# Hybrid encoder trunk: per-half buffers for the last 1/rms, VectorE evacuation of four FFN tiles, and later splits of one weight and four operands

## Chip, cores and metric

One NeuronCore of one Trainium2 chip runs the whole kernel in one launch. The metric is the device time of an execution in microseconds (us); times inside the program are counted from the start of the profiled span. TensorE is called PE in the rows, VectorE DVE, ScalarE ACT, GpSimd POOL; SP is the queue that issues most DMA transfers. PEld is TensorE's loading of weights.

## What is computed

Two encoder layers over 512 tokens of width 1024 in float32. Only the FFN and the last norm matter here (the reference, cut):

```python
for i in range(DEPTH):                      # DEPTH = 2
    ...                                     # norm, input projection, attention and SSD groups, output projection
    h = rms_norm(x, norm_ffn_w[i])
    g = jnp.einsum("bld,df->blf", h, w_gate[i])
    u = jnp.einsum("bld,df->blf", h, w_up[i])      # D_FF = 2816 = 22 tiles of 128
    x = x + jnp.einsum("blf,fd->bld", jax.nn.silu(g) * u, w_down[i])
return rms_norm(x, final_norm_w)
```

## The kernel before

All products are made in float32r from operands split in two: a high part `h` (a cast by ScalarE) and a low part (VectorE subtracts the high part from the source). A product a·b becomes three matmuls, hi·hi, hi·lo and lo·hi, so each weight chunk needs a `whi` (ACT, line 191) and a `wlo` (DVE, line 192). Weights stream through `Stream`: `next()` hands out one chunk and writes the splits of the two after it, and the load of the third, into the program. Two `wraw` buffers hold raw chunks, so the load of a chunk waits until the `wlo` of the chunk two before it has been made.

The 22 FFN tiles of a layer are worked in four phases, tiles 0 to 3, 4 to 9, 10 to 15 and 16 to 21. The first four (`PLAIN = 4`) are "plain": 24 matmuls of 512 columns for gate and 24 for up each, in PSUM banks a, s, t, s. Their evacuation is `evac`: VectorE multiplies gate by the token scale `rb` (1/rms spread over a tile), ScalarE applies SiLU, GpSimd multiplies the result by `rb` again, VectorE multiplies by up, and the hidden tile is split into `hid` (cast by ACT, line 1011, low part by DVE, line 1012). The tiles `gs` (tag e0) and `a_` (tag e1) have one buffer each. The other 18 tiles go in pairs by a seven-product scheme with sums of weight blocks and sums of the normed input. For that, still during the plain tiles, VectorE makes the normed input `xn` (line 1020, eight instructions), three operands `s11`, `s12`, `s22`, four sums in place (line 1051), and then four summed operands `ss1`, `ss2`, `sn4`, `ss3` (lines 1027 and 1028), which lie in the buffers `xh` and `xl` that the plain tiles' matmuls still read.

At the end of each phase come the down products: eight output tiles m = 0 to 7 in banks a and s by turns, each over the phase's hidden tiles; in the first phase that is 12 matmuls of 512 columns per m (lines 1112 to 1114), and then one add to x (DVE, line 1115).

A scheduler that works from its own times orders the instructions of each engine when the kernel is built; each engine then runs its list strictly in that order, and an instruction that waits holds all behind it. `tc.high_priority()` moves instructions forward in that order; `tc.issue_after(i)` puts them behind i.

The last norm (`Last`) works its last tile in two halves of 256 tokens. Each half's 1/rms is made by `rsqrt` on VectorE (eleven instructions on 128x2 elements, lines 290 to 296) and then applied by ACT (lines 407, 410) and DVE (412) to the output rows; eight DMAs of 256 KB write them out. The result tile of `rsqrt` takes its name as its tag, so two calls with one name share one buffer.

## Time and profile before

| | |
|---|---|
| median of 3 runs | 1213.37 us (1212.6 to 1213.63) |
| the profiled execution's own time | 1212.78 us |
| its span, first to last instruction | 1211.0 us |
| around the span | 1.78 us |
| TensorE busy in the span | 1190.3 us (98%) |
| VectorE, ScalarE, GpSimd busy | 902.2, 633.3, 149.8 us |
| mean granted TensorE clock | 0.995 of full speed |

Sums below are made against the profiled execution (1212.78 us), which lies 0.59 us below the median. A matmul's busy time in the rows overlaps that of the next one, so what TensorE loses is read from the distance of starts, not from the busy share.

### The profile page before, as it was taken

What the parts mean: (1) busy time and instruction counts of PE and PEld (TensorE: products, weight loads), DVE (VectorE), ACT (ScalarE), POOL (GpSimd) and SP (SyncE); (2) the same over time, 40 slices, a digit from 0 to 9 for tenths busy, and PEclk for the clock granted to TensorE, in tenths of its full rate; (3) what the DMA queues carried; (4) which work ended last, traced back from release to release, by engine and by line L of the source; (5) the groups of instructions that cost most, each with busy time, mean ns of one, the idle gap of its engine ahead of it and who ended that gap; (6) DMA issues with size and microseconds to landing.
All of it is one profiled execution on the core that took longest, in us unless ns stands there. A gap on an engine that the chain in (4) does not pass through costs nothing.

```text
span 1211.0 us, 19732 instructions
## 1 busy us (share of the span) xinstructions
PE 1190.3 (98%) x7720; PEld 1056.5 (87%) x7720; DVE 902.2 (75%) x1477; ACT 633.3 (52%) x1208; POOL 149.8 (12%) x140
## 2 busy tenths in 40 slices
PE   9999999999999999999999999999999999999996
PEld 7889887788899899899898888878879989989985
DVE  7999986568886676677779977866688857847842
ACT  5668775344444354254556876844335524533634
POOL 0202432012000000000211053401020000000011
PEclk9999999999999999999999999999999999999998
DMA  6221111225143233231433111312242432332121
GB/s 223 96 75 54 44 53 53 73 84 165 58 135 123 70 122 114 67 100 40 151 126 103 60 35 56 95 33 91 81 146 96 140 105 70 124 108 83 36 79 70
DMA packets 47534, 110.04 MB, mean 91 GB/s; under 512 B 5425, under 2 KB 5937, under 8 KB 47441
## 3 DMA queue, kind: packets, MB, share of 16 engines
q1 hardware_dynamic: 46720, 107.68, 28.0%
q8 instruction: 60, 0.98, 0.3%
q10 hardware_dynamic: 720, 1.11, 0.3%
q14 instruction: 34, 0.27, 0.1%
HBM read 104.44 MB, written 4.33 MB: 90 GB/s over the span
## 4 chain that ended last, share of the span: by engine, by line
PE 89%; DVE 5%; ACT 3%; DMA 1%; issue 1%; POOL 0%; SPq 0%; ACTq 0%; DVEq 0%; POOLq 0%
PE ps_a L1068 6%; PE ps_a L1067 6%; PE ps_a L1066 6%; PE ps_a L419 5%; PE ps_a L420 5%; PE ps_a L421 5%; PE ps_s L1112 3%; PE ps_s L1114 3%; PE ps_s L1113 3%; PE ps_a L1113 3%; PE ps_a L1112 3%; PE ps_a L1114 3%; PE ps_s L1068 3%; PE ps_s L1067 3%; PE ps_s L1066 3%; PE ps_t L729 3%
## 5 line engine op out<-in xcount | busy, mean ns | idle before, releaser
L191 ACT CAST whi<-wraw 128x512 fp32r<-128x512 f32 (+4 forms) x183 | 125.5, 714 | 211.6 <-PE ps_a L420 52.7
L191 ACT CAST whi<-sraw 128x1024 fp32r<-128x1024 f32 x126 | 131.7, 1050 | 141.0 <-DVE sraw L166 40.4
L192 DVE TENSOR_TENSOR wlo<-wraw,whi 128x512 fp32r<-128x512 f32 (+4 forms) x183 | 149.4, 831 | 54.2 <-ACT whi L191 53.1
L192 DVE TENSOR_TENSOR wlo<-sraw,whi 128x1024 fp32r<-128x1024 f32 x126 | 153.6, 1223 | 46.3 <-ACT whi L191 46.1
L328 POOL TENSOR_TENSOR ssq<-ssq,sqt 128x512 f32<-128x512 f32 x17 | 24.9, 1463 | 680.0 <-ACT sqt L325 679.3
L419 PE MATMUL ps_a<-xh,whi 128*128 128x512 f32 x272 | 107.2, 397 | 0.6 <-DVE x L834 0.3
L421 PE MATMUL ps_a<-xh,wlo 128*128 128x512 f32 x272 | 106.6, 392 | 0.0
L420 PE MATMUL ps_a<-xl,whi 128*128 128x512 f32 x272 | 106.3, 392 | 0.0
L166 DVE TENSOR_TENSOR sraw<-sraw 128x1024 f32<-128x1024 f32 x72 | 88.0, 1222 | 1.0
L1068 PE MATMUL ps_a<-ss,wlo 128*128 128x256 f32 x288 | 81.7, 284 | 0.0
L1066 PE MATMUL ps_a<-ss,whi 128*128 128x256 f32 x288 | 81.5, 283 | 0.0
L1067 PE MATMUL ps_a<-ss,whi 128*128 128x256 f32 x288 | 81.5, 283 | 0.0
L1068 PE MATMUL ps_a<-s,wlo 128*128 128x256 f32 x288 | 81.1, 283 | 0.0
L1067 PE MATMUL ps_a<-s,whi 128*128 128x256 f32 x288 | 81.1, 283 | 0.0
L1066 PE MATMUL ps_a<-s,whi 128*128 128x256 f32 x288 | 79.8, 283 | 0.0
L427 PE MATMUL ps_a<-whi,xh 128*128 128x256 f32 (+1 forms) x256 | 74.2, 291 | 0.1
L428 PE MATMUL ps_a<-wlo,xh 128*128 128x256 f32 (+1 forms) x256 | 73.9, 290 | 0.0
L429 PE MATMUL ps_a<-whi,xl 128*128 128x256 f32 (+1 forms) x256 | 71.9, 286 | 0.0
L1113 PE MATMUL ps_a<-hid,whi 128*128 128x512 f32 x176 | 68.9, 391 | 1.7 <-DVE hid L1012 1.7
L1112 PE MATMUL ps_s<-hid,whi 128*128 128x512 f32 (+1 forms) x182 | 70.0, 385 | 0.3 <-DVE a__3261 L1009 0.2
L1113 PE MATMUL ps_s<-hid,whi 128*128 128x512 f32 (+1 forms) x182 | 69.8, 384 | 0.0
L1114 PE MATMUL ps_s<-hid,wlo 128*128 128x512 f32 (+1 forms) x182 | 69.7, 383 | 0.0
(412 smaller groups left out, 3441.7 us busy)
## 6 DMA issues: line engine op xcount, KB each, us to landing
sraw<-in_w_gate SPq DMA_DIRECT2D x72, 256.0 KB, 3.3
sraw<-in_w_up SPq DMA_DIRECT2D x72, 256.0 KB, 4.0
wraw<-in_w_down SPq DMA_DIRECT2D x48, 384.0 KB, 3.2
wraw<-in_w_xbc SPq DMA_DIRECT2D x16, 512.0 KB, 3.2
wraw<-in_w_out SPq DMA_DIRECT2D x16, 512.0 KB, 3.3
wraw<-in_w_q SPq DMA_DIRECT2D x8, 512.0 KB, 3.5
wraw<-in_w_z SPq DMA_DIRECT2D x8, 512.0 KB, 3.3
wraw<-in_w_gate SPq DMA_DIRECT2D x8, 512.0 KB, 3.2
```

Of the source, the lines that this page charges most:

```text
L166: V.tensor_tensor(q[to], q[to], q[by], ALU.add)
L191: A.copy(hi[:, u], raw[:, u])
L192: (G if lo_pool else V).tensor_tensor(lo[:, u], raw[:, u], hi[:, u].bitcast(F32), ALU.subtract)
L419: T.matmul(ps, lhsT=wh, rhs=op.h[k], start=first, stop=False)
L420: T.matmul(ps, lhsT=wh, rhs=op.l[k], start=False, stop=False)
L421: T.matmul(ps, lhsT=wl, rhs=op.h[k], start=False, stop=last)
L1066: T.matmul(out, lhsT=wh[:, o:o + P], rhs=x_[:, 0, i], start=first and i + j == 0, stop=False, skip_group_check=True)
L1067: T.matmul(out, lhsT=wh[:, o:o + P], rhs=x_[:, 1, i], start=False, stop=False, skip_group_check=True)
L1068: T.matmul(out, lhsT=wl[:, o:o + P], rhs=x_[:, 0, i], start=False, stop=i == 3, skip_group_check=True)
L1112: T.matmul(ps[:, cols], lhsT=w1[:, o:o + P], rhs=h, start=f == a, stop=False)
L1113: T.matmul(ps[:, cols], lhsT=w1[:, o:o + P], rhs=g, start=False, stop=False)
L1114: T.matmul(ps[:, cols], lhsT=w2[:, o:o + P], rhs=h, start=False, stop=f == b - 1)
```

## The change

Four edits. The two last calls of `rsqrt` get a name, and so a buffer, each. In `evac`, up is multiplied by `rb` on VectorE (a new instruction from PSUM), GpSimd's product is gone, and VectorE multiplies the two in SBUF; `evac` runs under `high_priority`. The cast of the first down chunk of a layer (`late`) is put behind the cast `W.cast`, which at that point of the program is that of the third plain tile's hidden half. The four operands with a tag that begins with x (`ss1`, `ss2`, `sn4`, `ss3`) are put behind `W.low`, the low part of the fourth plain tile; the built program keeps that for their VectorE halves, while two of their casts on ScalarE stand ahead of the third tile's.

```diff
@@ -99,7 +99,7 @@
         return psum.tile([P, S], F32, name=f"ps_{tag}", tag=tag)
 
 
-    chunks, pairs = [], []
+    chunks, pairs, late = [], [], []
 
     def stream(src, n, lo=0, cut=WU):
 
@@ -130,6 +130,8 @@
                 for what in PRODUCTS:
                     chunks.append((len(pairs) - 1, what, None, WU))
             for m in range(KT):
+                if a == 0 and m == 0:
+                    late.append(len(chunks))
                 stream(w_down[l, m, :, a * P:b * P], (b - a) * P)
 
     class Stream:
@@ -188,7 +190,9 @@
                 lo = wp.tile([P, WU], F32R, name="wlo", tag="wlo", bufs=WB)
                 for a in range(0, n, KVDT if j == 0 else cut):
                     u = slice(a, min(a + (KVDT if j == 0 else cut), n))
-                    A.copy(hi[:, u], raw[:, u])
+
+                    with tc.issue_after(self.cast.ins) if j in late else nullcontext():
+                        A.copy(hi[:, u], raw[:, u])
                     (G if lo_pool else V).tensor_tensor(lo[:, u], raw[:, u], hi[:, u].bitcast(F32), ALU.subtract)
                 self.sp[j] = (hi, lo)
                 self.raw[j] = None
@@ -398,7 +402,7 @@
                 T.matmul(ms[:, c:c + 1], lhsT=q[:, c * P:(c + 1) * P], rhs=inv, start=False, stop=True)
             mm = small(nrm, 2, "mf")
             V.tensor_scalar(mm, ms[:, :2], EPS, None, ALU.add)
-            rt = rsqrt(nrm, mm, 2, "rfin")
+            rt = rsqrt(nrm, mm, 2, f"rfin{i}")
 
             def last(i, o, tp):
                 for c in range(2):
@@ -1002,14 +1006,14 @@
 
             def evac(f, pg, pu, rb):
                 gs = ff.tile([P, S], F32, name="gs", tag="e0")
+                a_ = ff.tile([P, S], F32, name="a_", tag="e1")
                 V.tensor_tensor(gs, pg, rb, ALU.mult)
+                V.tensor_tensor(a_, pu, rb, ALU.mult)
                 A.activation(gs, gs, AF.Silu)
-                G.tensor_tensor(gs, gs, rb, ALU.mult)
-                a_ = ff.tile([P, S], F32, name="a_", tag="e1")
-                V.tensor_tensor(a_, gs, pu, ALU.mult)
+                V.tensor_tensor(a_, a_, gs, ALU.mult)
                 ah, al = (t.rearrange("p a b -> p (a b)") for t in hidden(f))
-                A.copy(ah, a_)
-                V.tensor_tensor(al, a_, ah.bitcast(F32), ALU.subtract)
+                W.cast = A.copy(ah, a_)
+                W.low = V.tensor_tensor(al, a_, ah.bitcast(F32), ALU.subtract)
 
 
             ops, parts = {}, {}
@@ -1024,8 +1028,10 @@
 
             def operand(name, src, pool, tag):
                 t = pool.tile([P, 2, 4, 256], F32R, name=f"s{name}", tag=tag)
-                A.copy(t[:, 0], src)
-                V.tensor_tensor(t[:, 1], src, t[:, 0].bitcast(F32), ALU.subtract)
+
+                with tc.issue_after(W.low.ins) if tag[0] == "x" else nullcontext():
+                    A.copy(t[:, 0], src)
+                    V.tensor_tensor(t[:, 1], src, t[:, 0].bitcast(F32), ALU.subtract)
                 ops[name] = t
 
             for f in range(PLAIN):
@@ -1043,14 +1049,16 @@
                 if f == 0:
                     with tc.high_priority():
                         _, rb = norm.finish()
-                    evac(f, *pp, rb)
+                    with tc.high_priority():
+                        evac(f, *pp, rb)
                     scaled(rb)
                     for i, n in enumerate(("11", "12", "22")):
                         operand(n, parts[n], ff, f"s{i}")
                     for to, x_, y_ in (("22", "21", "22"), ("21", "11", "21"), ("11", "22", "11"), ("12", "12", "11")):
                         V.tensor_tensor(parts[to], parts[x_], parts[y_], ALU.add if to == "12" else ALU.subtract)
                 else:
-                    evac(f, *pp, rb)
+                    with tc.high_priority():
+                        evac(f, *pp, rb)
 
             for n, src, tag in (("s1", "22", "xh1"), ("s2", "11", "xl1"), ("n4", "12", "xh0"), ("s3", "21", "xl0")):
                 operand(n, parts[src], res, tag)
```

How the engines' lists change is shown at three places, all in the first layer; the second layer has the same rows. Line numbers of the changed kernel are 4 to 8 higher. The first place is VectorE's list from the second plain tile's hidden half to the down products, before. `wlo_3197`, `wlo_3228`, `wlo_3279` and `wlo_3299` are the low parts of down chunks m = 0, 1, 2, 3; `a__3190` and `a__3261` are the third and fourth plain tile.

```order
L1012 TENSOR_TENSOR hid_3028<-a__3120,hid_3028 128x512
L1051 TENSOR_TENSOR xn1_3032<-xn0_3031,xn1_3032 128x4x256
L192 TENSOR_TENSOR wlo_3279<-wraw_3231,whi_3278 128x512
L1051 TENSOR_TENSOR xn0_3031<-xn0_3031,xn1_3032 128x4x256
L1009 TENSOR_TENSOR a__3190<-gs_3186,ps_t_3155 128x512
L1005 TENSOR_TENSOR gs_3257<-ps_s_3195,rbc_3020 128x512
L1028 TENSOR_TENSOR ss2_3268<-xn1_3032,ss2_3268 128x1024
L1028 TENSOR_TENSOR ss1_3265<-xn0_3031,ss1_3265 128x1024
L1012 TENSOR_TENSOR hid_3192<-a__3190,hid_3192 128x512
L1028 TENSOR_TENSOR ss3_3274<-xn1_3032,ss3_3274 128x1024
L1009 TENSOR_TENSOR a__3261<-gs_3257,ps_s_3226 128x512
L192 TENSOR_TENSOR wlo_3299<-wraw_3282,whi_3298 128x512
```

There the low parts of m = 0 and 1 stand further up, that of m = 2 stands ahead of the operands, and those of m = 3 between them. The same place in the changed kernel (`a__3258` is the fourth plain tile):

```order
L196 TENSOR_TENSOR wlo_3197<-wraw_3160,whi_3196 128x512
L1011 TENSOR_TENSOR a__3258<-ps_s_3226,rbc_3020 128x512
L196 TENSOR_TENSOR wlo_3228<-wraw_3200,whi_3227 128x512
L1013 TENSOR_TENSOR a__3258<-a__3258,gs_3257 128x512
L1016 TENSOR_TENSOR hid_3192<-a__3258,hid_3192 128x512
L1034 TENSOR_TENSOR ss1_3265<-xn0_3031,ss1_3265 128x1024
L1034 TENSOR_TENSOR ss2_3268<-xn1_3032,ss2_3268 128x1024
L1034 TENSOR_TENSOR sn4_3271<-xn0_3031,sn4_3271 128x1024
L1034 TENSOR_TENSOR ss3_3274<-xn1_3032,ss3_3274 128x1024
L196 TENSOR_TENSOR wlo_3279<-wraw_3231,whi_3278 128x512
L196 TENSOR_TENSOR wlo_3299<-wraw_3282,whi_3298 128x512
L1123 TENSOR_TENSOR x0_2853<-x0_2853,ps_a_3277 128x512
```

All four operands now stand in one piece behind the fourth tile's low part, and the low parts of m = 2 and 3 stand behind all four.

The second place is TensorE's list at the start of the down products, before: `ps_a_3277` is m = 0, `ps_a_3317` is m = 2, `hid_3028` holds plain tiles 0 and 1, `hid_3192` tiles 2 and 3.

```order
L1112 MATMUL ps_a_3277<-hid_3028,whi_3196 128x512
L1113 MATMUL ps_a_3277<-hid_3028,whi_3196 128x512
L1114 MATMUL ps_a_3277<-hid_3028,wlo_3197 128x512
L1112 MATMUL ps_a_3317<-hid_3028,whi_3278 128x512
L1113 MATMUL ps_a_3317<-hid_3028,whi_3278 128x512
L1114 MATMUL ps_a_3317<-hid_3028,wlo_3279 128x512
L1112 MATMUL ps_a_3317<-hid_3028,whi_3278 128x512
L1113 MATMUL ps_a_3317<-hid_3028,whi_3278 128x512
L1114 MATMUL ps_a_3317<-hid_3028,wlo_3279 128x512
```

The first matmul with `wlo_3279` is there the sixth of this piece, and three matmuls of m = 0 stand even before the fourth tile's last ones. In the changed kernel no down matmul stands among the plain tiles; 28 of m = 0 to 3 come first, of which the last six are shown, and then the first with `wlo_3279` (`ps_s_3297` is m = 1, `ps_s_3337` m = 3):

```order
L1121 MATMUL ps_a_3277<-hid_3192,whi_3196 128x512
L1122 MATMUL ps_a_3277<-hid_3192,wlo_3197 128x512
L1121 MATMUL ps_s_3297<-hid_3192,whi_3227 128x512
L1122 MATMUL ps_s_3297<-hid_3192,wlo_3228 128x512
L1120 MATMUL ps_s_3337<-hid_3028,whi_3298 128x512
L1121 MATMUL ps_s_3337<-hid_3028,whi_3298 128x512
L1122 MATMUL ps_a_3317<-hid_3028,wlo_3279 128x512
L1120 MATMUL ps_a_3317<-hid_3028,whi_3278 128x512
L1121 MATMUL ps_a_3317<-hid_3028,whi_3278 128x512
```

The list behind that row holds 67 further matmuls of the phase, which all stand behind it.

The third place is ScalarE's list at the start of the first pair of the second phase, before. `whi_3414` is the chunk of the pair's first product, `e0` the copy that frees bank a for the third one.

```order
L191 CAST whi_3414<-sraw_3396 128x1024
L191 CAST whi_3433<-sraw_3396 128x1024
L1077 COPY e0_3450<-ps_a_3454 128x512
L191 CAST whi_3458<-sraw_3396 128x1024
L191 CAST whi_3487<-sraw_3402 128x1024
L191 CAST whi_3517<-sraw_3399 128x1024
L191 CAST whi_3546<-sraw_3405 128x1024
L1079 COPY e1_3451<-ps_s_3455 128x512
```

And in the changed kernel, where the copy stands three casts further back:

```order
L195 CAST whi_3414<-sraw_3396 128x1024
L195 CAST whi_3433<-sraw_3396 128x1024
L195 CAST whi_3458<-sraw_3396 128x1024
L195 CAST whi_3487<-sraw_3402 128x1024
L195 CAST whi_3517<-sraw_3399 128x1024
L1085 COPY e0_3450<-ps_a_3454 128x512
L195 CAST whi_3546<-sraw_3405 128x1024
L1087 COPY e1_3451<-ps_s_3455 128x512
```

On SP the load of down chunk 2 moves from among the twelve loads of the next phase's blocks (`sraw`) to behind them.

## Rows read from the trace of the kernel before

**Rows 1.** The page: busy time of each engine, and the chain that ended last.
```profile
PE 1190.3 (98%) x7720; PEld 1056.5 (87%) x7720; DVE 902.2 (75%) x1477; ACT 633.3 (52%) x1208; POOL 149.8 (12%) x140
...
PE 89%; DVE 5%; ACT 3%; DMA 1%; issue 1%; POOL 0%; SPq 0%; ACTq 0%; DVEq 0%; POOLq 0%
```

**Rows 2.** Timeline of PE: start, length (us), engine, line, output<-inputs, [idle before <-releaser].
```profile
290.06 0.39 PE L419 MATMUL ps_s<-xh,whi 128*128 128x512 f32 x1
...
301.16 0.39 PE L421 MATMUL ps_s<-xh,wlo 128*128 128x512 f32 x1
...
305.24 0.39 PE L1112 MATMUL ps_a<-hid,whi 128*128 128x512 f32 x1
306.49 0.50 PE L1113 MATMUL ps_a<-hid,whi 128*128 128x512 f32 x1 [0.85 <-DVE hid L1012]
...
311.46 0.39 PE L1113 MATMUL ps_a<-hid,whi 128*128 128x512 f32 x1
...
896.01 0.50 PE L1113 MATMUL ps_a<-hid,whi 128*128 128x512 f32 x1 [0.85 <-DVE hid L1012]
```

**Rows 3.** Timeline of DVE, first layer, plain FFN tiles.
```profile
277.23 0.69 DVE L1005 TENSOR_TENSOR gs<-ps_a,rbc 128x512 f32<-128x512 f32 x1 [2.34 <-ACT rbc L351]
...
288.19 0.68 DVE L1005 TENSOR_TENSOR gs<-ps_s,rbc 128x512 f32<-128x512 f32 x1
288.79 1.21 DVE L1028 TENSOR_TENSOR s<-xn,s 128x1024 fp32r<-128x1024 f32 x1
...
294.13 0.69 DVE L1009 TENSOR_TENSOR a__3120<-gs,ps_s 128x512 f32<-128x512 f32 x1 [1.19 <-POOL gs L1007]
```

**Rows 4.** Groups by line, DVE, 277 to 311: busy, mean ns of one.
```profile
L1020 DVE SCALAR_TENSOR_TENSOR xn<-x,par,rbc 128x512 f32<-128x512 f32 x8 | 6.4, 873 | 0.0
L1028 DVE TENSOR_TENSOR ss<-xn,ss 128x1024 fp32r<-128x1024 f32 x3 | 4.7, 1585 | 0.0
L1028 DVE TENSOR_TENSOR s<-xn,s 128x1024 fp32r<-128x1024 f32 x3 | 3.6, 1212 | 0.0
```

**Rows 5.** Timeline of POOL, the same tiles.
```profile
289.67 4.42 POOL L1007 TENSOR_TENSOR gs<-gs,rbc 128x512 f32<-128x512 f32 x1 [8.61 <-ACT gs L1006]
...
303.26 1.49 POOL L1007 TENSOR_TENSOR gs<-gs,rbc 128x512 f32<-128x512 f32 x1 [3.81 <-ACT gs L1006]
```

**Rows 6.** Timeline of ACT, the same tiles.
```profile
298.64 2.01 ACT L1027 CAST ss<-xn 128x1024 fp32r<-128x1024 f32 x2
301.76 0.62 ACT L1011 CAST hid<-a__3190 128x512 fp32r<-128x512 f32 x1 [1.11 <-DVE a__3190 L1009]
```

**Rows 7.** Timeline of the SP queue, second layer: one down weight load.
```profile
903.53 0.33 SPq L177 DMA_DIRECT2D wraw<-in_w_down  x1
```

**Rows 8.** Timeline of ACT: the cast that waited for that load.
```profile
906.30 0.62 ACT L191 CAST whi<-wraw 128x512 fp32r<-128x512 f32 x1 [3.73 <-DMA wraw<-in_w_down]
```

**Rows 9.** Timeline of all engines at the end of the program.
```profile
1202.34 1.22 ACT L410 ACTIVATE o<-o,rfin 128x512 f32<-128x512 f32 x2
...
1203.59 0.17 DVE L291 TENSOR_SCALAR rfin<-rfini 128x2 int32<-128x2 int32 x1 [2.50 <-ACT o L410]
...
1205.56 1.15 DVE L412 TENSOR_SCALAR o<-o,rfin 128x512 f32<-128x512 f32 x3
1205.62 0.62 ACT L407 ACTIVATE o<-ps_t,rfin 128x128 f32<-128x128 f32 x2 [2.06 <-DVE rfin L296]
1206.13 0.72 ACT L410 ACTIVATE o<-o,rfin 128x512 f32<-128x512 f32 x1
```

**Rows 10.** 1 us slices: PE, PEld, DVE, ACT, POOL busy, PEclk, DMA share, GB/s.
```profile
1201.00:1202.00 1.00, 0.00 (x0) 0.00 (x0) 0.09 (x1) 1.00 (x3) 0.00 (x0) 1.00 0.00 0
...
1205.00:1206.00 1.00, 0.00 (x0) 0.00 (x0) 0.90 (x5) 0.38 (x2) 0.00 (x0) 0.50 0.31 119
1206.00:1207.00 1.00, 0.00 (x0) 0.00 (x0) 0.70 (x3) 0.85 (x2) 0.00 (x0) 0.50 0.06 23
...
1209.00:1210.00 1.00, 0.00 (x0) 0.00 (x0) 0.00 (x0) 0.00 (x0) 0.00 (x0) 0.50 0.67 256
```

## Prediction, made before the run

> **What bounds the kernel now.** The page comes first: TensorE is busy 98% of the span and holds 89% of the chain that ended last [rows 1]. So an edit to another engine pays only where TensorE waits for it, or behind TensorE's last matmul. The second view is TensorE's timeline through the plain tiles and the first down products. Starts are 0.2265 us apart where nothing is waited for: 49 matmuls between the first two rows of [rows 2]. From 305.24 to 311.46 there are 20 matmuls, which need 20 x 0.2265 = 4.53 us and take 6.22: TensorE loses 1.69 us, and the rows name the low part of a hidden tile (line 1012) as what it waited for. The same wait of 0.85 us stands in the second layer [rows 2], so the stage loses about 3.4 us in all. That is the most the FFN edits can win. The third view is the end of the program: VectorE waits 2.50 us for ACT's last read of the first half's 1/rms before it may start the second half's [rows 9].
>
> **The end.** With a buffer of its own, the second `rsqrt` goes on at about 1201.1 instead of 1203.59 [rows 9]. Its chain (1203.59 to 1205.56) then ends near 1203.1, ahead of ScalarE, which is busy with the first half until 1202.34 + 1.22 = 1203.56. ScalarE's three last instructions took 1205.62 to 1206.85; they run from about 1203.46 and end at 1204.7, 2.15 us earlier. But the output must also be written. The first half's data ends at 1205.31 (a share of 0.31 in the slice from 1205), and the second half's takes a slice's 0.06 + 2 + 0.67 = 2.7 us of the DMA engines at full share [rows 10]. Started right behind the first half's, it ends at 1205.3 + 2.7 = 1208.0 instead of 1209.67. I take -1.65 us; the bounds are -2.2 (all of ScalarE's gain) and -1.2 (half a microsecond of gap left between the halves).
>
> **VectorE's load in the plain tiles.** Each tile gains one 512-element instruction, spaced 0.60 us (288.19 to 288.79 [rows 3]): +2.4 us a layer. It loses GpSimd's product, and with it what that did to VectorE: the mean of the operand split is 1585 ns for the three `ss`, which lie around GpSimd's work at 303.26, and 1212 ns for the three `s` [rows 4, 5], so 1.1 us; and VectorE's wait of 1.19 us for GpSimd's product of 4.42 us [rows 3, 5]. Together 2.3 us come back, so VectorE's load stays about even, and what decides is the order. The Trainium skill says the same of the two engines: GPSIMD Engine Reference, section Specifications, gives GpSimd's SBUF interfaces as shared with VectorE, with contention where VectorE has two SBUF inputs. The rows agree, with the 1585 against 1212 ns. By the rule alone VectorE's load would come out even or lighter and the stage could only win, up to 3.4 us; the next part says why the sum doesn't follow it.
>
> **Where the new order puts the down weights.** The chain in the first layer, by the spacings 0.60 (512 elements) and 1.13 (288.79 with 1.21 less the 0.08 by which rows overlap) for VectorE, 0.79 for the `xn` (873 ns less 0.08 [rows 4]), 0.52 and 0.95 for ScalarE's casts (0.62, and 2.01 for two, less 0.1 of overlap [rows 6]):
> - VectorE from 277.23: ten of 0.60, eight of 1.13 and the eight `xn` bring it to 277.23 + 6.0 + 9.0 + 6.3 = 298.6, and the third tile's product to 299.4 at most.
> - ScalarE has two operand casts ahead of the third tile's cast now. They overwrite `xl1`, which TensorE reads last 13 matmuls before the end of the fourth tile. That tile ends three matmuls earlier than before, since no down products stand in it: last start 301.16 - 0.68 = 300.48. So the casts start at 300.48 - 13 x 0.2265 + 0.39 = 297.9, the third tile's hidden cast ends at 300.45, `whi` of m = 0 at 301.0, that of m = 1 at 301.5, SiLU of the fourth tile at 302.0; two more operand casts follow, and the fourth hidden cast ends at 304.45.
> - VectorE then: fourth low part from 304.46, next slot 305.06; four operand splits of 1.13 up to 309.6; `wlo` of m = 2, 0.68, ready at 310.3.
> - TensorE starts the down products at 300.71 and waits for `whi` of m = 0 to 301.0. The 28 matmuls ahead of the first with `wlo` of m = 2 would end at 300.71 + 28 x 0.2265 = 307.05. It goes on at 310.3: 3.25 us late, plus about 0.1 that a restart costs. Nothing else is ready in its list.
>
> So TensorE loses 3.35 us a layer in place of 1.69: **+1.66 a layer, +3.3 for two**. Bounds: from below, the chain cannot start before TensorE's last gate or up matmul ends (300.87); two slots of 0.60, a product of 0.68, a cast of 0.62, a slot of 0.60, four of 1.13 and 0.68 bring it to 309.2, 2.15 us late, +0.46 a layer. From above, as many restarts as before (0.3 us more) give +2.0. The changed SP order and the first down cast cost nothing of their own: m = 2's load is issued after `wlo` of m = 0 at about 301.8 and its cast is done near 305.2, over four microseconds before its `wlo` has its turn.
>
> **Sum.** +3.3 - 1.65 = +1.7 us on the profiled 1212.78, which lies 0.59 below the median; on the median, 1215.0 us. That is +0.13%; about 0.2% (2.4 us) is what a measurement of this kernel can tell from no change.
>
> **Rivals.**
> - *The copy that frees bank a becomes late* (+0.74 a layer or so). In the first pair it stands behind three more casts, and those behind VectorE sums that stand behind the late down weights. From 310.3: two loads in a row, 2.8 us each from the issue to the start of the cast (903.53 to 906.30 [rows 7, 8]), each with 0.62 and 0.68 behind it, give the cast of m = 6 done at 317.8; then about 9.4 us of VectorE slots, three casts of 0.95 and the copy of 0.59 end near 330.6. TensorE reaches the third product at 310.3 + 68 x 0.2265 + 48 x 0.12 (half as many columns) = 331.4. The margin is 0.8 us, and each 0.1 us on a load counts twice: at loads of 3.2 it is gone, at 3.6 it costs about 0.75 a layer. That gives +1.5: 1216.5. Chance 0.18.
> - *The clock falls in the new wait.* The trace shows the granted clock at 0.50, the lower level of 1.2 GHz, with TensorE idle since 1200.4, and 1.00 still in the slice from 1201 [rows 10]. The new wait of about 3 us in one piece lies between the waits of about a microsecond that the kernel has now and the idle end. If TensorE then runs at half rate for as long as it waited, it loses half of 3 us a layer: 1218.0. TensorE: Matmul & The Clock Gate, Part 1, in the Trainium skill, has idling close the gate, which speaks against this change; no row here shows a wait of this length with dense work on both sides. Chance 0.10.
> - *Faster: TensorE doesn't wait.* If the low part of m = 2 were ready when the 28 matmuls end, the FFN edits would win the whole 3.4 us and the end 1.65: 1208.3. It decides at four splits of 1.13 - 3.25 / 4 = 0.3 us each, where the fastest row has 1.13. Chance 0.07.
> - *The end pays nothing*, because another transfer or wait takes the place of the 2.50 us: 1216.7. The share of 0.06 in the slice from 1206 [rows 10], DMA engines idle for want of data, speaks against it. Chance 0.05.
> - *A smaller FFN loss*, down to the lower bound: +0.9 - 2.2 to +0.9 - 1.65, 1212.1 to 1212.6 at the end. Chance 0.08, no measurable change.
>
> **Chances and range.** My forecast holds 0.52; its own range is 1212.9 to 1216.5 (+0.9 to +4.0 for the two layers, with -1.2 to -2.2 at the end), and about a fifth of it lies over 1215.8. Slower by over 0.2%: 0.18 + 0.10 + 0.05 + 0.10 = 0.43; faster 0.07; no measurable change 0.50. The range 1212.3 to 1217.6 takes in the unknowns but most of the clock and the faster case.
>
> **What would show it.** VectorE's low part of m = 2 around 310 and 899 or so, ScalarE's operand casts ahead of it, and TensorE with one wait near 3 us just before the first matmul with it (line 1122), released by VectorE; the waits for line 1012's hidden parts gone; at the end no wait of VectorE for ACT and the outputs written without a gap. Wrong if TensorE shows no such wait, if the wait is followed by matmuls at twice the spacing, or if the first pair's third product waits too.

## Result, and the profile after

The changed kernel took 1220.4 us (median of 5 runs, 1217.95 to 1221.04) against 1213.37: a ratio of 1.0062, 95% interval [1.0051, 1.0073], so 6 to 9 us slower. The forecast was 1215.0 with a range of 1212.3 to 1217.6. It gave 0.43 to a kernel slower by over 0.2% and 0.50 to no measurable change; the size lies outside its range.

The page of the kernel after, its row of busy times, as [rows 1]:

```profile
PE 1194.3 (98%) x7720; PEld 1053.6 (87%) x7720; DVE 901.9 (74%) x1485; ACT 633.6 (52%) x1208; POOL 130.7 (11%) x132
```

The engines do as much as before: VectorE has eight instructions more and the same sum, GpSimd eight less. Only TensorE is busy for 4.0 us longer, with the same 7720 matmuls. That is the first sign that matmuls became slower, since a wait doesn't count as busy.

TensorE's timeline in the first layer's first down products, as [rows 2], and in the second layer; the line of the third matmul of a set is 1122 now:

```profile
306.51 0.40 PE L1121 MATMUL ps_s<-hid,whi 128*128 128x512 f32 x1
309.38 0.53 PE L1122 MATMUL ps_a<-hid,wlo 128*128 128x512 f32 x1 [2.48 <-DVE wlo L196]
309.72 0.62 PE L1120 MATMUL ps_a<-hid,whi 128*128 128x512 f32 x1
310.14 0.63 PE L1121 MATMUL ps_a<-hid,whi 128*128 128x512 f32 x1
...
313.37 0.40 PE L1122 MATMUL ps_s<-hid,wlo 128*128 128x512 f32 x1
...
903.62 0.80 PE L1122 MATMUL ps_a<-hid,wlo 128*128 128x512 f32 x1 [2.48 <-DVE wlo L196]
```

The wait is where the prediction put it, of the predicted kind. Behind it the matmuls start 0.42 us apart for 3.4 us, then 0.23. The 1 us slices of the same stretch, PE alone (busy time and count, granted clock, DMA share, GB/s), with one of the second layer, say why:

```profile
308.00:309.00 1.00, 0.00 (x0) 1.00 0.00 0
309.00:310.00 1.00, 0.61 (x2) 0.86 0.00 0
310.00:311.00 1.00, 1.00 (x4) 0.50 0.59 106
...
313.00:314.00 1.00, 1.00 (x5) 0.93 0.00 0
...
905.00:906.00 1.00, 1.00 (x4) 0.50 0.90 332
```

The granted clock is 1.00 through the wait and falls to 0.50 (1.2 GHz) just after TensorE has begun again, for three to four microseconds, in both layers. The Trainium skill, TensorE: Matmul & The Clock Gate, Part 1, has idling close the gate; the trace agrees, with the fall behind the idling.

VectorE's timeline just before that wait ends, which answers to [rows 3]:

```profile
303.49 0.69 DVE L1016 TENSOR_TENSOR hid<-a__3258,hid 128x512 fp32r<-128x512 f32 x1 [0.88 <-ACT hid L1015]
304.10 2.35 DVE L1034 TENSOR_TENSOR ss<-xn,ss 128x1024 fp32r<-128x1024 f32 x2
...
307.51 1.22 DVE L1034 TENSOR_TENSOR ss<-xn,ss 128x1024 fp32r<-128x1024 f32 x1
308.65 1.29 DVE L196 TENSOR_TENSOR wlo<-wraw,whi 128x512 fp32r<-128x512 f32 x2
```

Four splits of 1.13 us lie between the last hidden low part and the weights' low parts of m = 2 and 3, while TensorE idles. The end, VectorE, ScalarE and the SP queue, as [rows 9]:

```profile
1208.94 0.17 DVE L294 TENSOR_SCALAR rfin1i<-mf 128x2 int32<-128x2 int32 x1
1209.15 0.17 DVE L295 TENSOR_SCALAR rfin<-rfin1i 128x2 int32<-128x2 int32 x1
...
1209.94 4.47 SPq L417 DMA_DIRECT2D out_t<-o  x8
...
1211.68 0.61 ACT L411 ACTIVATE o<-ps_t,rfin 128x128 f32<-128x128 f32 x2
1212.18 0.72 ACT L414 ACTIVATE o<-o,rfin 128x512 f32<-128x512 f32 x1
```

VectorE's second `rsqrt` goes on at once, where it waited 2.50 us [rows 9]. Three marks cut an execution into stages: ScalarE's copy of the 1/rms row (`rbc`), which comes once in each mixer and once in each FFN, the last sum of the residual, and the end of the span. The marks of before, then those of after, in the timelines of ACT and DVE:

```profile
276.61 0.59 ACT L351 COPY rbc<-ps_m 128x512 f32<-128x512 f32 x1 [2.98 <-PE ps_m L349]
625.29 0.59 ACT L351 COPY rbc<-ps_m 128x512 f32<-128x512 f32 x1 [0.52 <-PE ps_m L349]
866.14 0.59 ACT L351 COPY rbc<-ps_m 128x512 f32<-128x512 f32 x1 [2.98 <-PE ps_m L349]
1198.35 0.42 DVE L1115 TENSOR_TENSOR x<-x,ps_s 128x256 f32<-128x256 f32 x1
```

```profile
275.61 0.59 ACT L355 COPY rbc<-ps_m 128x512 f32<-128x512 f32 x1 [2.98 <-PE ps_m L353]
629.03 0.59 ACT L355 COPY rbc<-ps_m 128x512 f32<-128x512 f32 x1 [0.23 <-PE ps_m L353]
869.84 0.59 ACT L355 COPY rbc<-ps_m 128x512 f32<-128x512 f32 x1 [2.98 <-PE ps_m L353]
1206.58 0.42 DVE L1123 TENSOR_TENSOR x<-x,ps_s 128x256 f32<-128x256 f32 x1
```

The first layer's FFN stage (from the first mark to the second) takes 353.42 us for 348.68, +4.74; the second layer's (from the third to the last sum) 336.74 for 332.21, +4.53; what follows 11.12 (1217.7 - 1206.58) for 12.65 (1211.0 - 1198.35), -1.53. So the end paid nearly what it should, and the FFN lost 4.6 us a layer in place of the forecast 1.66. The three together are +7.7, and the spans differ by 6.7: the rest is the first layer's mixer, which the change doesn't touch, and which took 241.24 us before and 240.27 after (from the mixer's own mark, at 35.4 and 35.3 us, to the first one above). That 1.0 us is the clock's, too. In the profiled execution of before the granted clock fell to 0.50 for 3.4 us near 24 us, and TensorE took the delay past the mixer's mark; in that of after it stayed at 1.00 there. Over the profiled executions of all fourteen kernels the mixer's time goes with that fall: 240.3 to 240.4 us in the four without that fall, 241.0 to 241.5 in the eight with it, 242.5 to 242.6 in the two (e11, e12) in which it lasted 6.8 us. The second layer's mixer takes 240.8 to 240.9 in all.

The wait and the clock don't fill 4.6 us a layer. Busy time by line and shape, PE, 330 to 625 us, shows the third part. Rows of before, then of after:

```profile
L1068 PE MATMUL ps_a<-ss,wlo 128*128 128x256 f32 x144 | 40.8, 284 | 0.0
L1068 PE MATMUL ps_a<-s,wlo 128*128 128x256 f32 x136 | 38.3, 283 | 0.0
...
L1114 PE MATMUL ps_a<-hid,wlo 128*128 128x512 f32 x72 | 28.0, 389 | 0.0
```

```profile
L1076 PE MATMUL ps_a<-ss,wlo 128*128 128x256 f32 x144 | 40.7, 283 | 0.0
L1076 PE MATMUL ps_a<-s,wlo 128*128 128x256 f32 x136 | 37.8, 280 | 0.0
...
L1122 PE MATMUL ps_a<-hid,wlo 128*128 128x512 f32 x72 | 28.4, 395 | 0.0
```

At a clock of 1.00 throughout, each matmul on `hid` takes 6 ns more (its starts are 0.2333 us apart, not 0.2271), each on `s11`, `s12` and `s22` 3 ns less (0.1178, not 0.1199). Those on `ss` and `sn` change by half a nanosecond at most, and the mixer's by no more than a nanosecond. In the built programs the place of `hid` and the `s` is 32 bytes further on than before: the second half's 1/rms got a place in the pool of small tiles, and all that is allocated behind that pool moved. `ss` and `sn` lie ahead of it.

### The profile page after: what moved, and what is told of

It is laid out like the page before. It is cut to its first block, busy times and chain, and to the rows that moved or that the text cites. A ratio compares the mean times of both kernels' runs of the same rounds, so it can differ in the third digit from the quotient of the medians.

```text
span 1217.7 us, 19733 instructions
## 1 busy us (share of the span) xinstructions
PE 1194.3 (98%) x7720; PEld 1053.6 (87%) x7720; DVE 901.9 (74%) x1485; ACT 633.6 (52%) x1208; POOL 130.7 (11%) x132
## 4 chain that ended last, share of the span: by engine, by line
PE 89%; DVE 4%; ACT 3%; issue 1%; DMA 1%; POOL 0%; SPq 0%; ACTq 0%; DVEq 0%; POOLq 0%
PE ps_a L1076 6%; PE ps_a L1074 6%; PE ps_a L1075 6%; PE ps_a L423 5%; PE ps_a L424 5%; PE ps_a L425 5%; PE ps_a L1122 3%; PE ps_a L1120 3%; PE ps_a L1121 3%; PE ps_s L1122 3%; PE ps_s L1120 3%; PE ps_s L1121 3%; PE ps_s L1076 3%; PE ps_s L1075 3%; PE ps_s L1074 3%; PE ps_t L733 3%
## 5 line engine op out<-in xcount | busy, mean ns | idle before, releaser
L1122 PE MATMUL ps_a<-hid,wlo 128*128 128x512 f32 x176 | 71.1, 404 | 5.0 <-DVE wlo L196 5.0
```

The costliest lines, as they stand in the source:

```text
L1122: T.matmul(ps[:, cols], lhsT=w2[:, o:o + P], rhs=h, start=False, stop=f == b - 1)
```

## Experiments

Theory 1: the loss has three parts, the wait behind four splits, the half clock that often follows it, and the moved starts. Its rival at each step stands in what was expected of the run. Where a stage is named, it is measured between the marks above; "loss" is TensorE's, the sum of what its starts lie further apart than 0.227 us in the plain tiles, the first down products and the first pair (0.12 for 256 columns). The table has the profiled execution of each kernel: both FFN stages, what follows the last sum, and the median of all its runs with its ratio.

| kernel | FFN, layer 0 | FFN, layer 1 | end | us | ratio to before, 95% |
|---|---|---|---|---|---|
| before | 348.68 | 332.21 | 12.65 | 1213.37 | |
| after | 353.42 | 336.74 | 11.12 | 1220.40 | 1.0062 [1.0051, 1.0073] |
| e1 end edit alone | 350.14 | 333.46 | 11.11 | 1213.26 | 1.0003 [0.9993, 1.0013] |
| e2 32 bytes alone | 350.34 | 333.47 | 12.71 | 1213.88 | 1.0016 [1.0007, 1.0025] |
| e3 after, 32 bytes more | 351.50 | 333.35 | 11.09 | 1214.53 | 1.0016 [1.0006, 1.0025] |
| e5 after, places kept | 351.93 | 333.91 | 11.03 | 1216.69 | 1.0035 [1.0022, 1.0048] |
| e6 e5, splits not held | 349.30 | 332.91 | 11.65 | 1212.57 | 1.0001 [0.9991, 1.0011] |
| e7 e6, cast not held | 349.67 | 332.86 | 11.12 | 1214.08 | 1.0014 [1.0005, 1.0023] |
| e8 end edit, places kept | 349.00 | 332.19 | 11.11 | 1210.82 | 0.9984 [0.9975, 0.9993] |
| e9 e5, wait filled | 350.35 | 333.90 | 11.04 | 1214.29 | 1.0015 [1.0005, 1.0025] |
| e11 low parts first | 348.81 | 332.65 | 11.05 | 1211.33 | 0.9991 [0.9982, 1.0001] |
| e12 e11, s moved | 345.36 | 328.74 | 11.12 | 1204.63 | 0.9935 [0.9920, 0.9950] |

The kernel before took 1212.3 to 1212.6 us (medians) beside the experiments, and their ratios are against these.

Two things in the table need care. The first layer's stage scatters: e8, and e10 below, have the FFN of before instruction for instruction, and took 349.00 and 349.61 us there for 348.68, while their second layers took 332.19 and 332.20 for 332.21. So a difference of under 1 us is read from the second layer. And the time outside the span is 2.1 to 2.2 us (medians) in every kernel with the FFN edits (after, e3, e5, e6, e7, e9, e11, e12), for 1.7 to 1.8 in the others: 0.4 us that no stage shows, and whose cause stays open.

**e1 and e2: the end edit alone, and 32 bytes alone.**

```diff
-            rt = rsqrt(nrm, mm, 2, "rfin")
+            rt = rsqrt(nrm, mm, 2, f"rfin{i}")
```

> Only the end edit (the two 1/rms a place each), nothing of the FFN edits. The new place makes the pool of small tiles 32 bytes larger, so every tile allocated after it, hid and s11, s12, s22 among them, starts 32 bytes further on. Theory 1 (where a matmul's moving operand starts sets the matmul's spacing): the end wins 1.5 us as in the trace of after, and the FFN stage shows the same spacings as after, 0.2333 us instead of 0.2267 for the 528 down matmuls of a layer (+3.5 us) and 0.1177 instead of 0.1200 for the 648 matmuls on s11, s12, s22 (-1.5 us), so +4.0 us for two layers and +2.5 us in all. Theory 2 (the spacings of after come from its FFN edits or from the run): spacings as before, and the kernel is 1.5 us faster than before.

```diff
-        t = pool.tile([P, n], F32, name=name + "t", tag=f"rst{n}")
+        t = pool.tile([P, n + (8 if n == 2 else 0)], F32, name=name + "t", tag=f"rst{n}")[:, :n]
```

> Before with 32 unused bytes behind the small tile rfint, and no other edit: the same instructions in the same order, all tiles behind it 32 bytes further on. Theory 1: spacings 0.2333 and 0.1177 as in after, +4.0 us against before. Theory 2: no difference to before.

The kernel with nothing but 32 unused bytes has the slower and the faster matmuls of after. Its rows by line and shape, PE, 330 to 625 us:

```profile
L1068 PE MATMUL ps_a<-s,wlo 128*128 128x256 f32 x136 | 37.9, 280 | 0.0
...
L1114 PE MATMUL ps_a<-hid,wlo 128*128 128x512 f32 x72 | 28.5, 395 | 0.0
```

So theory 2 fell in kind: no instruction is changed or reordered here. In size theory 1 was too high: the two FFN stages lose 1.66 and 1.26 us (e1: 1.46 and 1.25) where 2.0 each was expected, and the whole +1.5 us (0.8 to 3.0) where 4.0 was. About a quarter of a microsecond a layer of the difference lies in the 864 matmuls on `ss` and `sn`, which start 0.2 to 0.5 ns closer than before; the rest isn't explained. In e1 the 2.7 us of the two stages eat the 1.54 that the end wins, and the kernel is no faster.

**e3: the whole change and 32 more bytes.** On the kernel after:

```diff
-        t = pool.tile([P, n], F32, name=name + "t", tag=f"rst{n}")
+        t = pool.tile([P, n + (8 if n == 2 else 0)], F32, name=name + "t", tag=f"rst{n}")[:, :n]
```

> After with 32 more unused bytes behind rfint, so that hid and s11, s12, s22 start at 32 bytes past a multiple of 64 again, as before the change (96 past a multiple of 128 where it was 32). Theory 1: spacings back at 0.2267 and 0.1200, 4.0 us less than after, which leaves the wait of 2.5 us and the half clock behind it: about 1216.4 us. Theory 2: as after, about 1220.4 us.

The spacings are 0.2291 and 0.1180, not 0.2271 and 0.1199: theory 1 was wrong that the start within 64 bytes is what counts, but right that the place sets it; 1.9 ns times 528 less 1.9 ns times 648 is -0.2 us, so by this sum the run shows the wait and the clock nearly alone. At 1214.53 us it is 1.9 us faster than theory 1 had it, and it shows more than it was made for. Both layers wait alike, for 2.58 us in one piece, for VectorE's `wlo`. The slices behind the wait, of the first layer and of the second:

```profile
311.00:312.00 1.00, 1.00 (x4) 0.50 0.96 361
...
903.00:904.00 1.00, 1.00 (x6) 1.00 0.97 344
```

The clock fell behind the first wait and not behind the second, with the same wait, the same matmuls and about the same DMA traffic in these slices. The stages differ by it: +2.82 and +1.14.

**e5: the whole change, no other tile moved.**

```diff
-            rt = rsqrt(nrm, mm, 2, f"rfin{i}")
+            rt = rsqrt(W.pool if i else nrm, mm, 2, f"rfin{i}")
```

> The whole change, but the second half's 1/rms lies in the FFN's pool, behind everything else in it, so that no other tile moves. Theory 1 (the loss of after is the wait, the half clock behind it in most cases, and the moved operands): spacings 0.2271 and 0.1200 as before, the wait of 2.5 us at the weights' low part of m = 2 as in after; a layer loses 1.3 us against before where the clock stays at 1.00 behind the wait and 3.0 where it falls to 0.50; the end wins 1.5. Together +1.1 to +4.5 us against before. Theory 2 (places don't matter): as after, +7 us.

The spacings are 0.2272 and 0.1200, and the wait is there in both layers (2.6 us each). Again the clock fell to 0.50 in the first layer, and stayed at 1.00 in the second:

```profile
311.00:312.00 1.00, 1.00 (x4) 0.50 0.57 131
...
904.00:905.00 1.00, 1.00 (x6) 1.00 0.79 188
```

The stage with the fall loses 3.25 us against before, the one without 1.70. In the latter TensorE's loss is 3.37 us, in place of 1.69. (Both stages lose more than e3's, by 0.43 and 0.56, so e3's places weren't quite neutral.) At +4.2 us (2.7 to 5.8) the whole is at the upper end of what was expected; theory 2's +7 is outside the interval.

**e9: the wait filled.** e5 with ten matmuls on operands at hand ahead of the one that waits:

```diff
...
+                        if a == 0 and m == 3:
+                            with tc.high_priority(), tc.issue_after(mid.ins):
+                                fl = bank("m")
+                                for j in range(FILL):
+                                    T.matmul(fl, lhsT=w1[:, :P], rhs=h, start=j == 0, stop=j == FILL - 1)
```

(`FILL` is 10, and `mid` the last matmul ahead of the wait.)

> As e5 (the whole change, no other tile moved), with ten more matmuls of 512 columns on operands at hand into an unused bank, put into TensorE's list just ahead of the first matmul that waits for the weights' low part of m = 2. They take 10 x 0.227 = 2.3 us of the wait of 2.6 and change no result. Theory 1 (TensorE's idling in the wait is what halves its clock in some executions): granted clock 1.00 behind the wait in every execution's stage, FFN stage +1.7 us a layer against before always, so 1.2 us less than e5 as it is in the median, and a narrower spread. Rival (the clock falls for something else in this stage): as e5, or up to 4.5 us more where the matmuls don't fit into the wait.

TensorE's timeline and the slices behind the wait, first layer:

```profile
305.87 2.43 PE L1128 MATMUL ps_m<-hid,whi 128*128 128x512 f32 x10
308.62 0.50 PE L1123 MATMUL ps_a<-hid,wlo 128*128 128x512 f32 x1 [0.32 <-DVE wlo L196]
```

```profile
309.00:310.00 1.00, 1.00 (x6) 1.00 0.37 49
310.00:311.00 1.00, 1.00 (x6) 1.00 0.92 328
```

The matmul that waited comes no earlier in its stage, but the clock stays at 1.00 in both layers, and the stages lose 1.67 and 1.69 us. The kernel is 2.4 us faster than e5 by the medians, twice the 1.2 that was expected; its ten runs lie within 2.0 us, e5's five within 2.3, so a narrower spread isn't shown. Two stages at 1.00 might be luck where two of six unfilled ones were, but the other runs say the same: the mean granted clock of a run is 0.993 to 0.995 in e5's five and 0.995 to 0.997 in e9's ten. So in this stretch TensorE's idling is what brings the clock down, and matmuls without a use keep it up. That the wait alone costs 1.7 us a layer is shown by three stages now (e5's second and both of e9).

**e6, e7: which edit makes the wait.** e6 is e5 without the `issue_after` of the four operands; e7 is e6 without that of the first down cast.

```diff
-                with tc.issue_after(W.low.ins) if tag[0] == "x" else nullcontext():
+                with nullcontext():
```

> As e5, but the four operands' splits are no longer issued behind the last hidden low part. Theory 1 (this delay puts four splits between the fourth low part and the weights' low part of m = 2, and that is the wait): no wait over 1 us in the down stage, clock at 1.00 there, and the stage loses at most the 1.7 us that it lost before: -1.5 us against before from the end, down to -4.9 if the small waits go too. Rival: the wait comes from VectorE's added instruction in each tile or from the cast held back, and stays: +1 us or more against before.

```diff
-                    late.append(len(chunks))
+                    pass
```

> As e6, and the first down cast is no longer issued behind the last hidden cast either: the end and VectorE's evacuation alone. If holding that cast back is worth something (ScalarE's hidden casts come earlier), the down stage waits up to 1.7 us a layer more than in e6, as it did before the change; if not, as e6.

In e6 the wait of 2.6 us and the fall of the clock are gone, as expected, so the delay of the four splits makes them. The gain isn't there, though: a wait for the weights' low part comes earlier, now that of m = 0. TensorE's waits from 290 to 320 us, in e6 and then in e7:

```profile
PE ps_a L1122 <- DVE wlo L196: 1.0, 1, 1.0
```

```profile
PE ps_a L1120 <- ACT hid L1015: 1.1, 1, 1.1
PE ps_s L1120 <- DVE gs L1010: 1.0, 1, 1.0
```

TensorE's loss in the first layer is 2.28 us in e6 and 2.67 in e7, against 1.69 before: +0.59 and +0.98, which the stages repeat (+0.62, +0.99). The first layer scatters by as much, but the second lost 0.70 and 0.65 against before. So in none of these orders (e5, e6, e7) was VectorE's evacuation free. 0.5 us of e6's missing gain is its end, 11.65 for 11.1, and isn't explained. Whether holding back the cast is worth something stays open: e7's first layer is 0.4 us longer than e6's, its second isn't, and the medians differ by 1.5 us.

**e8: the end edit alone, places kept.** On the kernel before:

```diff
-            rt = rsqrt(nrm, mm, 2, "rfin")
+            rt = rsqrt(W.pool if i else nrm, mm, 2, f"rfin{i}")
```

> Only the end edit, the second half's 1/rms in the FFN's pool so that no other tile moves. Theory 1: FFN stage as before, -1.5 us against before; beside e1, which had the same edit and moved tiles, 1 to 3 us less. Theory 2 (places don't matter): as e1, no difference to before.

1.7 us faster (0.8 to 3.0), the end 11.11. The same edit lost all of that in e1 to 32 bytes.

**e11: the low parts first.** e5, with the four operands issued once the weights of m = 3 are split:

```diff
-                    (G if lo_pool else V).tensor_tensor(lo[:, u], raw[:, u], hi[:, u].bitcast(F32), ALU.subtract)
+                    self.low = (G if lo_pool else V).tensor_tensor(lo[:, u], raw[:, u], hi[:, u].bitcast(F32), ALU.subtract)
...
-            for n, src, tag in (("s1", "22", "xh1"), ("s2", "11", "xl1"), ("n4", "12", "xh0"), ("s3", "21", "xl0")):
-                operand(n, parts[src], res, tag)
...
+                    if a == 0 and m == 1:
+                        for n, src, tag in (("s1", "22", "xh1"), ("s2", "11", "xl1"), ("n4", "12", "xh0"), ("s3", "21", "xl0")):
+                            operand(n, parts[src], res, tag)
```

(`W.low` is then the low part of m = 3's weights.)

> As e5 (the whole change, no other tile moved), but the four operands' splits are issued behind the weights' low part of m = 3, and so behind that of m = 2, instead of behind the last hidden low part. Theory 1 (the wait is the four splits ahead of the low part of m = 2, and nothing else of the change costs time): that low part is ready near 305.5 in place of 309, before TensorE reaches it at 307; no wait over 1 us and the clock at 1.00; the stage wins what it lost before the change, 1.0 to 1.7 us a layer, and the end 1.6: 3.6 to 5 us less than before. Rival (VectorE has too much to do in this stretch in any order): the wait moves to the low part of m = 4, or to the sums that free the banks, and the kernel is no faster than e8 (-1.7).

VectorE's timeline and TensorE's, first layer:

```profile
307.86 0.69 DVE L196 TENSOR_TENSOR wlo<-wraw,whi 128x512 fp32r<-128x512 f32 x1 [0.74 <-ACT whi L195]
308.47 2.35 DVE L1034 TENSOR_TENSOR ss<-xn,ss 128x1024 fp32r<-128x1024 f32 x2
...
313.01 0.68 DVE L1121 TENSOR_TENSOR x<-x,ps_a 128x512 f32<-128x512 f32 x1
```

```profile
313.84 0.47 PE L1118 MATMUL ps_a<-hid,whi 128*128 128x512 f32 x1 [0.33 <-DVE x L1121]
...
331.28 0.39 PE L1072 MATMUL ps_a<-ss,whi 128*128 128x256 f32 x1 [0.29 <-ACT e L1083]
```

The long wait and the half clock are gone, with VectorE's extra instruction and all four splits still in place: theory 1 held for these. What TensorE loses in the first layer is 1.81 us, no less than before, spread over small waits: for the sum that frees a bank, which now stands behind the splits (313.84), and for the copy that frees bank a in the first pair (331.28), a rival of the prediction. In the second layer the stage is 0.44 us longer than before. So the 3.6 to 5 us of theory 1 didn't come, and the rival expected here was right about the gain: -1.1 us (-2.2 to +0.1) is no more than e8.

**e4, e10 and e12: the starts.** e4 gives the three places of `hid` and of the `s` starts of their own, by longer tiles of which a shifted slice is used.

```diff
-                    hid[f // 2] = ff.tile([P, 2, 4, 256], F32R, name="hid", tag=f"a{i}")
+                    o = (28, 4, 16)[i]
+                    hid[f // 2] = ff.tile([P, 2048 + 32], F32R, name="hid", tag=f"a{i}")[:, o:o + 2048].rearrange("p (i a b) -> p i a b", i=2, a=4, b=256)
...
```

(The tiles of the `s` are lengthened and shifted in the same way.)

> Before with the three places of hid and those of s11, s12, s22 shifted each by its own amount: they start at 16, 48 and 96 bytes past a multiple of 128 (before: all at 32; after: all at 64). No work is left out. Theory 1: the spacing of the matmuls differs from place to place, as the start does; if what counts is the start within 64 bytes, the third place (96, that is 32 past a multiple of 64) shows 0.2267 and 0.1200 as before, and 16 and 48 show other values, between 0.2133 (512 columns at 2.4 GHz) and 0.24 for 512 columns. Theory 2: all at 0.2267 and 0.1200.

In the order of the expectation the spacings were 0.2305, 0.2321 and 0.2335 us on `hid`, and 0.1175, 0.1197 and 0.1144 on the `s`: all differ, as theory 1 has it, but the third place, at 96, isn't back at 0.2271. Since e3's 96 gave 0.2291, the start within 128 bytes isn't what counts either.

e10 measures it by itself, with matmuls in the pattern of the down products behind the last output:

```diff
+    def series(name, n, mv, st):
+        ps = psum.tile([P, S], F32, name=f"ps_{name}", tag="a")
+        for j in range(24):
+            f = j // 3 % 2 if n == 512 else j // 3 % 4
+            w = (wh, wh, wl)[j % 3][:, st + (j // 3) * P:st + (j // 3 + 1) * P]
+            o = mv + (0, 1024, 0)[j % 3] + f * n
+            T.matmul(ps[:, :n], lhsT=w, rhs=mt[:, o:o + n], start=j == 0, stop=j == 23)
```

> Before with 64 series of 24 matmuls added behind the last output, on tiles of their own, which only measure: the moving operand starts 0 to 240 bytes further in steps of 16 (512 and 256 columns), the stationary one 0 to 112, and then the moving one 512 to 3584 bytes further. Its time is longer by these, some 220 us. Theory 1 (the start sets the spacing): the spacing goes with the start, 0.227 at 0 and 0.233 at 32 bytes for 512 columns, 0.120 and 0.118 for 256, as the hid and s tiles of before and e2 had it. Rival (it is the pair of moving and stationary starts, or the distance between them): moving the stationary operand alone changes the spacing as well.

The spacing of a series is from the start of its first matmul with `mwl` to that of its eighth, over 21. The first series of 512 columns, PE's timeline, has (1228.81 - 1224.05) / 21 = 0.2267:

```profile
1224.05 0.39 PE L1129 MATMUL ps_m<-mt,mwl 128*128 128x512 f32 x1
...
1228.81 0.39 PE L1129 MATMUL ps_m<-mt,mwl 128*128 128x512 f32 x1
```

All of them, in us (the granted clock is 1.00 throughout):

```
bytes further      0      16     32     48     64     80     96     112
moving, 512 col.   .2267  .2314  .2333  .2333  .2295  .2310  .2338  .2310
  (128 to 240)     .2324  .2333  .2338  .2329  .2333  .2348  .2333  .2267
moving, 256 col.   .1195  .1186  .1171  .1186  .1181  .1195  .1200  .1133
  (128 to 240)     .1181  .1186  .1171  .1195  .1133  .1195  .1181  .1171
stationary, 512    .2286  .2267  .2333  .2333  .2333  .2319  .2343  .2333
stationary, 256    .1195  .1186  .1186  .1176  .1133  .1190  .1176  .1200
moving by 512, 1024, ... 3584:  512 col. .2267 to .2271,  256 col. .1200
```

The values at 0, 32 and 64 bytes are those of before (0.2271 and 0.1199), of after and e2 (0.2333 and 0.1178) and of e3 (0.2291 and 0.1180), to within 0.7 ns. (The pair at 0 and 0 was measured twice for 512 columns, as .2267 and .2286, so a nanosecond or two is no difference.) But moving the stationary operand alone changes the spacing as well, so the rival has it: both starts count, not the moving one alone. Whether it is only the distance between the two wasn't tested, since no series moves both. The table hints at it: 16 bytes on the stationary side give the 0.2267 of 240 on the moving side, and 64 give the 0.1133 of 192, as if the distance counted within 256 bytes. But e4's third place of `hid`, 64 bytes on within 256, has 0.2335 where 64 has 0.2295 here, so that isn't the whole rule either. Moves by multiples of 512 bytes change nothing. For 512 columns no start was better than that of before; for 256 columns 112 and 192 bytes give 0.1133.

e12 uses this: e11 with `s11`, `s12` and `s22` 192 bytes further on.

```diff
-                t = pool.tile([P, 2, 4, 256], F32R, name=f"s{name}", tag=tag)
+                if pool is ff:
+                    t = pool.tile([P, 2048 + 64], F32R, name=f"s{name}", tag=tag)[:, 48:48 + 2048].rearrange("p (i a b) -> p i a b", i=2, a=4, b=256)
+                else:
+                    t = pool.tile([P, 2, 4, 256], F32R, name=f"s{name}", tag=tag)
```

> As e11, and the operands s11, s12 and s22 start 192 bytes further, in places of their own that are 256 bytes longer; hid stays. No work is left out. Theory 1 (the start sets the spacing, as the added series of e10 had it: 0.1133 us at 192 bytes for 256 columns, and s22 of e4, whose start was the same, 0.1144): 648 matmuls a layer at 0.1133 to 0.1144 in place of 0.1200, 3.6 to 4.3 us a layer, 7 to 9 us less than e11. Rival (places don't matter for the whole): as e11.

By line and shape, PE, 330 to 625 us:

```profile
L1077 PE MATMUL ps_a<-s,wlo 128*128 128x256 f32 x136 | 37.4, 277 | 0.0
...
L1123 PE MATMUL ps_a<-hid,wlo 128*128 128x512 f32 x72 | 28.0, 389 | 0.0
```

The matmuls on the `s` take 277 ns for 283, the stages 3.45 and 3.91 us less than in e11, and the kernel 1204.63 us: 6.7 less than e11, 0.65% faster than before. That is a little under the 7 to 9 expected, since the mean spacing was 0.1151 and not 0.1133 to 0.1144. It is the fastest kernel of the study, and most of what makes it so, 6.7 of 7.8 us, has nothing to do with the change.

## Why the prediction was wrong, point by point

- **The end, -1.65.** Right: -1.53 in after, -1.54 in e8, by the mechanism given: VectorE's wait for ScalarE is gone, and the output ends earlier.
- **"VectorE's load stays about even, and what decides is the order".** Right: 902.2 us busy before, 901.9 after.
- **The new order in the plain tiles, "TensorE loses 3.35 us a layer in place of 1.69".** Right in place, releaser and size: 3.37 in place of 1.69 where the clock held (e5, second layer), and e9's stages lose 1.67 and 1.69 more than before's. The prediction's VectorE chain put the low part of m = 2 at 310.3; it came at 309.3 in an execution whose FFN had begun 1.0 us earlier.
- **The step that failed first: "The clock falls in the new wait", given 0.10 as a rival and nothing in the sum.** It fell in four of the six waits of this length that the profiles show (both of after, one each of e3 and e5). The loss was sized well, at half of 3 us: 3.25 - 1.70 = 1.55 us a layer, by e5's two layers. The chance was wrong. The prediction argued from [rows 10], where the clock was still at 1.00 in the slice in which TensorE had stopped, that a wait of 3 us might pass. The slices of after show that this is no argument: the clock reads 1.00 through the whole wait, and falls once TensorE has begun again. The prediction also says that no row shows such a wait with dense work on both sides, but the trace of before has a shorter one, near its start. TensorE's timeline there, and one of the slices behind it:

```profile
23.43 1.05 PE L334 MATMUL ps_m<-inv,ssq 128*128 128x1 f32 x8 [1.14 <-DVE ssq L328]
24.34 0.58 PE L419 MATMUL ps_t<-xh,whi 128*128 128x512 f32 x1
```

```profile
25.00:26.00 1.00, 1.00 (x3) 0.50 0.33 131
```

A wait of 1.14 us and eight matmuls of one column, between matmuls of 256 and 512 columns, were followed by 3.4 us at 0.50. These rows spoke for the rival, and they were there to be read.
- **The step that failed next: "The end", costed by its wait alone.** The new place moved `hid` and the `s` by 32 bytes. The prediction priced each buffer's effect on order and waits and took the spacing of a matmul, 0.2265 from [rows 2], as given. It cost 1.46 and 1.25 us in e1's two stages, together nearly twice what the edit wins at the end, and no rival named it.
- **The sum by stages.** First layer: 1.70 + 1.55 + 1.46 = 4.71, measured 4.74. Second: 1.70 + 1.55 + 1.25 = 4.50, measured 4.53. That the first layer fits so well is in part luck, since it scatters by 0.9 us; the second, which doesn't, fits as well. The stages and the end as measured are +7.7, 0.4 comes outside the span, a term that the prediction didn't have, and the 1.0 us that the clock took near 24 us in the execution of before comes off: 7.1, the difference of the two profiled executions (1219.85 - 1212.78), and +7.0 by the medians.
- **The rival "the copy that frees bank a becomes late".** It did not come in after, whose TensorE waits for nothing in the pair phases. It came in e11, with 0.5 and 0.7 us in the two layers.
- **The rivals on the faster side.** "The end pays nothing" and "TensorE doesn't wait" are out by the rows above.

What stays open: why the clock fell behind some of the waits and not behind others just like them; and by what rule the starts of the two operands set the spacing. The Trainium skill, SBUF — State Buffer, Specifications, gives 16-byte cachelines with a penalty for each cross to a new one; all starts here are multiples of 16 bytes from each other and differ nevertheless, so this alone doesn't explain it.

## What to carry to other kernels

A wait of TensorE has two prices, its length and what the clock takes back behind it: where a change joins small waits into one long one, put the half clock into the sum, not among the rivals, look in the trace of before for a place where the clock already falls, and ask for filler matmuls or another order (e9, e11). Before a tile is added, look at what it moves: with operands that are read thousands of times, 32 bytes were worth 1.3 to 1.7 us a layer here, and a chosen start 3.5 to 3.9. And an edit that looks free should be tried alone: e1 and e8 are the same edit, and only one of them is faster.

## What the runs showed that was not expected

- The spacing of matmuls at a granted clock of 1.00 depends on where the operands start: 0.2267 to 0.2348 us for 512 columns and 0.1133 to 0.1200 for 256, for moves in steps of 16 bytes (e10). The directions differ: at 32 bytes 512 columns are 2.9% slower and 256 columns 2.0% faster.
- After a wait of 2.5 to 2.6 us the clock either fell to 0.50 for three to four microseconds, once TensorE was busy again, or not at all, in one and the same execution (e3, e5). Near 24 us it fell in ten of fourteen profiled executions: in before's behind a wait of 1.14 us, and not in after's behind one of 1.15.
